# Expert weights in runs of 16384 bytes through 2 MB ring slots

## The chip, the cores and the metric

The kernel runs on one core of one Trainium2 chip. The metric is device time in microseconds, the median of three runs; lower is better. Times inside the program count from the start of the profiled span.

## The reference

One batch of 256 tokens of width 1024 goes through two blocks in float32. The first block is an RMS norm, a mixer (an mLSTM in chunks beside a pooled branch) and a mixture of experts; the second is attention and a gated delta rule side by side and a dense feed-forward. The change lies in the mixture of experts, which comes down to this:

```
logits = xt @ w_router + b_router                  # 256 tokens, 32 experts
top_vals, top_idx = top_k(logits, 4)               # each token goes to 4 experts
gate = min(xb @ w_gate[e] + b_gate[e], 7)          # w_gate[e], w_up[e], w_down[e]: 1024 x 1024 f32
up   = clip(xb @ w_up[e] + b_up[e], -7, 7)
y    = (gate * sigmoid(1.702 * gate) * (up + 1)) @ w_down[e] + b_down[e]
out  = sum over a token's experts of its gate weight * y
```

Three matrices of 4 MB for each of 32 experts make 384 MB of weights, and every byte is read once.

## The kernel before

All large weights come through a ring of slots in on-chip memory (class `Ring`, L25 to L89). A load is one entry of `jobs`, 1 MB for the expert weights. `order` (L39) gives a list of slot pools, and `add` (L42) hands each load the next pool of that list. `fill` (L47) issues loads strictly in the order of the list, all from SP's queue (L53): when the pool of the next load has no free slot, `fill` returns, and no later load is issued either, whatever is free elsewhere. `take` (L65) gives the oldest loaded piece to its user, and `refill` (L58), called in program order right behind the piece's last user, frees the slot and calls `fill` again. So the order of SP's loads is fixed when the program is built, and a load can wait on SP only for the last reader of the slot that it reuses.

Before the change there are nine pools: pool 0 with four slots of 2112 columns, pool 1 with eight of 2048, and seven pools of one slot of 2048, which are opened when the mixer's memory comes free (`open_late`, L859). Together that is 19 slots of 1 MB, and 156672 bytes of each partition. The pools are visited in a cycle of 19, so a load always takes the slot that the load 19 places before it had.

`plan_stream` (L482) lists the loads: ten of the mixer's input matrix and four of its output matrix, then the experts' in the order in which TensorE uses them: gate 0, up 0, gate 1, up 1, down 0, gate 2, up 2, down 1, and so on, four loads for each matrix. I number the experts' loads from load 0 (the first quarter of gate 0) to load 384 (the last quarter of down 31 comes as two halves). Expert 6's gate is loads 68 to 71, its up loads 72 to 75.

A load (`add_rows`, L78) takes 256 rows of a matrix, two neighbouring rows to a partition: a run of 8192 bytes in memory for each of 128 partitions. So the rows that one matmul contracts are every second row of 256, and the activations are arranged to match: `xn` is written with a stride at L829, `n2p` holds the norm's weights in that order (L226, L258), and `swiglu` writes with the same stride (L1262, L1268).

`experts` (L985) runs over the 32 experts. For each pair it gathers the tokens by one-hot matmuls (`group`, L1010; ps_x in the profile); for each expert it multiplies by gate and up (`up`, L1047; ps_g and ps_u), passes the result through `swiglu` on VectorE and ScalarE, transposes it (ps_t), multiplies by down one expert later (`down`, L1074; ps_y) and scatters the sums back. One load feeds four fp32 matmuls of 128x512, which the profile counts as eight.

Of the kernel before, what the change touches and what calls it, by code (L numbers as in the profile page):

```python
# [26 lines left out]
class Ring:  # L27

    def __init__(self, nc, sizes):
        self.nc, self.sizes, self.pools = nc, sizes, {}
        self.cols = (SLOT,) + (2048,) * (1 + LATE)
        self.jobs, self.tiles, self.sent, self.taken, self.freed = [], {}, 0, 0, 0
        self.where, self.held = [], [0] * len(sizes)
        self.limit = 1 << 30

    def order(self, cycle):
        self.cycle, self.at = cycle, 0  # L39

    def add(self, *pieces):
        self.where.append(self.cycle[self.at % len(self.cycle)])  # L42
        self.at += 1
        self.jobs.append(pieces)

    def fill(self, most=1 << 30):
        while self.sent < min(len(self.jobs), most, self.limit):  # L47
            i = self.where[self.sent]
            if i not in self.pools or self.held[i] == self.sizes[i]:
                return  # L50
            t = self.pools[i].tile([128, self.cols[i]], F32, tag="w", name="w")
            for view, src in self.jobs[self.sent]:
                self.nc.sync.dma_start(out=view(t), in_=src)  # L53
            self.held[i] += 1
            self.tiles[self.sent] = t
            self.sent += 1

    def refill(self):  # L58

        self.held[self.where[self.freed]] -= 1  # L60
        self.freed += 1
        self.fill()

    def take(self):
        t = self.tiles.pop(self.taken)  # L65
        self.taken += 1
        return t

    def add_cols(self, w, c0, n, kpt, k_total, cut=1):

# [6 lines left out]

    def add_rows(self, w):  # L78

        self.add((lambda t: t[:, :w.shape[0] // 128 * w.shape[1]], w.rearrange("(p i) c -> p (i c)", p=128)))  # L80

    def add_two_cols(self, w, c0, c1, n, kpt, k_total):
        for k0 in range(0, k_total, kpt):
# [9 lines left out]
class Kernel:  # L93
# [122 lines left out]
    def load_late(self):  # L216
        a, c = self.a, self.c
        self.param_rows("pe", ("norm2", a["norm2_g"].rearrange("o (k p) -> (o k) p", p=128), 8),
                        ("normmix", a["norm_mix_2"].rearrange("o (k p) -> (o k) p", p=128), 8),
                        ("normffn", a["norm_ffn_2"].rearrange("o (k p) -> (o k) p", p=128), 8),  # L220
                        ("normf", a["normf_g"].rearrange("(k p) -> k p", p=128), 8),
                        ("gdnn", a["gdn_norm_2"].rearrange("o (k p) -> (o k) p", p=128), 1))

        self.n2rows = self.rows.tile([4, 256], F32, name="n2rows")
        self.nc.sync.dma_start(out=self.n2rows, in_=a["norm2_g"].rearrange("o (j c) -> (o j) c", j=4))
        self.n2p = c.tile([128, 4, 2], F32, name="n2p")  # L226
# [23 lines left out]
    def param_cols(self, name, psp, tag):  # L250
# [3 lines left out]
        self.nc.vector.tensor_copy(self.pt[name], ps[:, :n])  # L254
        if name == "pb":
            ps = psp.tile([128, 512], F32, tag=tag, name="ps_p")
            for i in range(2):
                self.nc.tensor.transpose(ps[:, 4 * i:4 * i + 4], self.n2rows.rearrange("j (p i) -> j i p", i=2)[:, i, :],  # L258
                                         self.ident[:4, :4])
            self.nc.vector.tensor_copy(self.n2p, ps[:, 0:8].rearrange("p (i j) -> p j i", i=2))  # L260
# [221 lines left out]
    def plan_stream(self):  # L482
        a, r = self.a, self.ring
        if self.stop == "b2":
            return self.plan_stream2()
        r.order([0] * RING[0] + [1] * RING[1])
        w_in = a["w_in"][0]
        for c0, n in ((2048, 520), (0, 512), (512, 512), (1024, 512), (1536, 512)):
            r.add_cols(w_in, c0, n, 4, KD, 2 if c0 == 2048 else 1)
# [3 lines left out]
        if self.stop == "p1":  # L493
            return

        n = RING[0] + RING[1]
        first = [r.cycle[(r.at + i) % n] for i in range(n)]
        r.order(first[:n - 4] + list(range(2, 2 + MID)) + first[n - 4:] + list(range(2 + MID, 2 + LATE)))
# [9 lines left out]
        for e in range(E):  # L508
            if e + 1 < E:
                gu("w_gate", e + 1)  # L510
                gu("w_up", e + 1)
            if e + 1 < E:
                gu("w_down", e)
            else:
                w = a["w_down"][0, e]
                for k0 in range(0, D - 256, 256):
                    r.add_rows(w[k0:k0 + 256])
                for i in range(2):
                    r.add((lambda t: t[:, :D], w[D - 256:].rearrange("(p i) c -> i p c", i=2)[i]))
        if self.stop == "moe":  # L520
            return

# [23 lines left out]
    def mixer(self, block1):  # L546
        nc, tc, a = self.nc, self.tc, self.a
        v, g_ = nc.vector, nc.gpsimd
        with ExitStack() as ctx:
# [428 lines left out]
    def experts(self):  # L978
        nc, tc, a, x = self.nc, self.tc, self.a, self.x
        v = nc.vector  # L980
        with ExitStack() as ctx:
# [28 lines left out]
            def group(g):  # L1010
# [11 lines left out]
                for k in range(KD):  # L1022
                    ps = psx.tile([128, 512], F32, tag="x", name="ps_x")
                    for tb in range(2):
                        self.mm(ps[:, 0:GR * CAP], xn[:, tb, k * 128:(k + 1) * 128],
                                oh[:, tb].rearrange("p e s -> p (e s)"), start=tb == 0, stop=tb == 1)
                    self.act(xt[:, k, :], ps[:, 0:GR * CAP], scale=self.n2p[:, k // 2, k % 2:k % 2 + 1])
# [145 lines left out]
    def overflow_block(self, xn, e, psx, psg, psy, pst):  # L1173
# [16 lines left out]
        for k in range(KD):  # L1190
            for tb in range(2):
                self.mm(ps[:, k, :], xn[:, tb, k * 128:(k + 1) * 128], oh[:, tb, :], start=tb == 0, stop=tb == 1)
            self.act(xt[:, k, :], ps[:, k, :], scale=self.n2p[:, k // 2, k % 2:k % 2 + 1])
# [5 lines left out]

        def load(name, k):  # L1200
            w = q.tile([128, D], F32, tag="xg", name="ow")
            k0 = k // 2 * 256
            nc.sync.dma_start(out=w, in_=a[name][0][ds(e, 1), k0:k0 + 256, :].rearrange(
                "o (p i) c -> i p (o c)", i=2)[k % 2])
            return w

        gu = []
        for name, bn, tag, place in (("w_gate", "b_gate", "g", "gg"), ("w_up", "b_up", "u", "sc")):
# [11 lines left out]
            v.tensor_tensor(out=self.pairs(t), in0=self.plain(ps), in1=self.plain(b), op=OP.add)  # L1220
            gu.append(t)
        gg = gu[0]
        self.swiglu(gg, *gu, paired=True)
# [22 lines left out]
    def pairs(self, x):  # L1246

        return x.rearrange("p (a i q) -> p a q i", a=2, i=2)

    def plain(self, x):  # L1250
        return x.rearrange("p (a q i) -> p a q i", a=2, i=2)

    def swiglu(self, gg, pg, pu, paired=False):


        v = self.nc.vector
        t = self.mow.tile([128, 512], F32, tag="sg", name="sg", bufs=1)

        if paired:
# [5 lines left out]
        if paired:  # L1265
            v.tensor_scalar(out=t, in0=pu, scalar1=7.0, scalar2=-7.0, op0=OP.min, op1=OP.max)
        else:
            v.tensor_scalar(out=self.pairs(t), in0=self.plain(pu), scalar1=7.0, scalar2=-7.0, op0=OP.min, op1=OP.max)  # L1268
        v.scalar_tensor_tensor(out=gg, in0=t, scalar=1.0, in1=gg, op0=OP.add, op1=OP.mult)


# [834 lines left out]
```

## Time and profile before

| | |
|---|---|
| median of three runs | 1653.11 us (1653.06 to 1653.57) |
| the profiled execution's own time | 1652.3 us |
| its span | 1650.6 us |
| TensorE busy | 1567.6 us, 95% of the span |
| loads on SP's DMA queue | 506.01 MB, mean 308 GB/s over the span |
| mixer | 0 to about 125 us |
| experts | about 125 to 1054 us |
| second block | 1054 us to the end |

The span is cut into 40 slices of 41.3 us on the page. A digit is the busy share of an engine in tenths, and the GB/s line tells what the 16 DMA engines moved. Waits are put down to what came last; a wait of TensorE's weight load (PEld) for "DMA w" is one for a weight that has not landed.

### The profile page before, as it was taken

To read this page: it belongs to the slowest core of one execution; us is meant where nothing else is said; L and a number is where in the kernel's file an instruction comes from. 1 tells how busy PE (TensorE), PEld (TensorE's weight loads), DVE (VectorE), ACT (ScalarE), POOL (GpSimd) and SP (SyncE) were. 2 spreads that over 40 slices of the span, in tenths; PEclk is the share of its full clock that TensorE was granted. 3 is DMA by queue.
4 is the path that set the end of the run, shared out by engine and by line. 5 is a ranking of instruction groups with operands and counts; after the bars stand their busy time and mean duration, and the time that the engine had idled before them with its cause. 6 is when DMAs were issued, how large, how long until landed. Compare 5 with 4: busy or idle time off the path is not lost. (4 is left out here: it accounts for less than half of the span.)

```text
span 1650.6 us, 22396 instructions
## 1 busy us (share of the span) xinstructions
PE 1567.6 (95%) x8810; PEld 950.9 (58%) x8811; DVE 695.4 (42%) x1437; ACT 524.9 (32%) x1151; POOL 54.8 (3%) x124
## 2 busy tenths in 40 slices
PE   8999999999999999999999998799999999999997
PEld 8783333333333333333323322489888999989996
DVE  6862212212121212122121121388875376777775
ACT  4562111111111111111111110256663356565554
POOL 0100000000000000000000010000111010000000
PEclk9999999999999999999999999999999999999999
DMA  8878999999999999999999999644343333556551
GB/s 285 305 307 310 408 418 421 421 422 421 420 422 420 421 421 422 421 420 421 421 421 421 421 421 421 271 131 155 124 153 103 103 120 137 179 166 202 182 187 69
DMA packets 119235, 508.31 MB, mean 308 GB/s; under 512 B 10364, under 2 KB 33717, under 8 KB 70101
## 3 DMA queue, kind: packets, MB, share of 16 engines
q1 hardware_dynamic: 117284, 506.01, 77.8%
q8 instruction: 71, 1.16, 0.3%
q10 hardware_dynamic: 1840, 0.82, 0.2%
q14 instruction: 40, 0.32, 0.1%
HBM read 505.74 MB, written 1.05 MB: 307 GB/s over the span
## 5 line engine op out<-in xcount | busy, mean ns | idle before, releaser
L349 DVE TENSOR_TENSOR lo<-w,hi 128x512 fp32r<-128x512 f32 (+2 forms) x380 | 257.3, 691 | 56.9 <-PE ps_d L109 30.6
L1081 DVE COPY ht<-ps_t 128x512 f32<-128x512 f32 x32 | 22.1, 692 | 596.5 <-PE ps_t L1079 596.5
L109 PE MATMUL ps_y<-w,ht 128*64 128x512 f32 x1024 | 230.1, 597 | 29.8 <-DVE ht L1081 25.1
L106 ACT ACTIVATE hi<-w 128x512 fp32r<-128x512 f32 (+2 forms) x380 | 232.1, 628 | 74.8 <-PE ps_d L109 67.2
L109 PE MATMUL ps_g<-w,xg 128*64 128x512 f32 x1024 | 238.3, 600 | 6.1 <-DMA w<-in_w_gate_dram 4.9
L109 PE MATMUL ps_u<-w,xg 128*64 128x512 f32 x1024 | 238.0, 600 | 2.9 <-DMA w<-in_w_up_dram 2.8
L109 PEld LDWEIGHTS ps_y<-w,ht 128*64 128x64 f32 x1024 | 69.2, 136 | 170.0 <-issue 113.6
L106 ACT ACTIVATE xg<-ps_x,n2p 128x128 f32<-128x128 f32 x128 | 47.0, 368 | 334.3 <-PE ps_x L109 334.0
L109 PEld LDWEIGHTS ps_g<-w,xg 128*64 128x64 f32 x1024 | 67.1, 136 | 135.2 <-issue 101.0
L109 PEld LDWEIGHTS ps_u<-w,xg 128*64 128x64 f32 x1024 | 66.1, 136 | 116.6 <-issue 96.3
L109 PEld LDWEIGHTS ps_x<-oh,xn 128*128 128x128 f32 x512 | 68.7, 190 | 78.2 <-issue 64.7
L106 ACT ACTIVATE y<-ps_y 64x512 f32<-64x512 f32 x64 | 37.9, 592 | 186.7 <-PE ps_y L109 186.1
L109 PE MATMUL ps_x<-oh,xn 128*128 128x128 f32 x512 | 86.9, 294 | 0.8 <-DVE oh L1016 0.8
L106 ACT ACTIVATE sg<-gg 128x512 f32<-128x512 f32 x32 | 20.1, 629 | 200.4 <-DVE gg L1262 200.3
L1110 DVE TENSOR_TENSOR x<-x,ps_x 128x512 f32<-128x512 f32 x64 | 43.9, 686 | 91.9 <-PE ps_x L109 91.9
L109 PE MATMUL ps_d<-hnh,hi 128*128 128x256 f32 x448 | 77.7, 295 | 0.8 <-ACT hi L106 0.5
L109 PE MATMUL ps_d<-hnh,lo 128*128 128x256 f32 x448 | 71.5, 281 | 3.2 <-DVE lo L349 3.1
L109 PE MATMUL ps_d<-hnl,hi 128*128 128x256 f32 x448 | 71.1, 281 | 0.0
L109 PE MATMUL ps_x<-y,sc 128*128 128x512 f32 x128 | 59.2, 605 | 11.1 <-ACT y L106 11.1
L109 PEld LDWEIGHTS ps_d<-hnh,hi 128*128 128x128 f32 x448 | 61.5, 189 | 3.5 <-ACT hi L106 0.6
L109 PEld LDWEIGHTS ps_d<-hnh,lo 128*128 128x128 f32 x448 | 60.7, 188 | 4.0 <-DVE lo L349 3.8
L109 PEld LDWEIGHTS ps_d<-hnl,hi 128*128 128x128 f32 x448 | 60.8, 188 | 0.2
(435 smaller groups left out, 2079.3 us busy)
## 6 DMA issues: line engine op xcount, KB each, us to landing
w<-in_w_down_dram SPq DMA_DIRECT2D x137, 1024.0 KB
w<-in_w_gate_dram SPq DMA_DIRECT2D x128, 1024.0 KB
w<-in_w_up_dram SPq DMA_DIRECT2D x128, 1024.0 KB
w<-in_w_in_dram SPq DMA_DIRECT2D x40, 1024.0 KB
w<-in_w_up_dram SPq DMA_DIRECT2D x44, 512.0 KB
w<-in_w_out_dram SPq DMA_DIRECT2D x8, 1024.0 KB
w<-in_w_branch_gdn_dram SPq DMA_DIRECT2D x4, 1024.0 KB
w<-in_w_branch_fox_dram SPq DMA_DIRECT2D x4, 1024.0 KB
```

The source lines that it names most:

```text
L106: self.nc.scalar.activation(out=out, in_=in_, func=func, **kw)
L109: self.nc.tensor.matmul(out, lhsT=lhsT, rhs=rhs, start=start, stop=stop, **kw)
L349: nc.vector.tensor_tensor(out=lo[:, :n], in0=src, in1=hi[:, :n].bitcast(F32), op=OP.subtract)
L1081: v.tensor_copy(ht, ps)
L1110: v.tensor_tensor(out=o, in0=o, in1=ps, op=OP.add)
```

## The change

The 384 MB now go through slots of two sizes. Pool 1 has four slots of 4096 columns (2 MB) instead of eight of 2048, pools 2, 3 and 4 one slot of 4096 each, pool 5 one of 2048, and pool 0 stays with four of 2112. That is the same 156672 bytes: seven wide slots and five narrow ones. A wide load brings 512 rows, four neighbouring rows to a partition, as runs of 16384 bytes; its two halves are handed out one after the other, and the slot is free when both have been used. Where the next slot is a narrow one, the same 512 rows come as two loads of 8192-byte runs. All activations follow the new order of rows (stride four instead of two).

The visiting order is now a list written out, `MOE_RING`: its second list is gone through once, then its first list again and again. Each list has 24 entries: 14 wide and 10 narrow, 38 MB. Numbering by megabytes as before, a wide load has two numbers.

```diff
-    def order(self, cycle):
-        self.cycle, self.at = cycle, 0
+    def order(self, cycle, first=()):
+        self.cycle, self.first, self.at, self.part = cycle, first, 0, 0
+    def at_pool(self):
+        n = len(self.first)
+        return self.first[self.at] if self.at < n else self.cycle[(self.at - n) % len(self.cycle)]
+    def wide(self, i):
+        return self.cols[i] > SLOT
     def add(self, *pieces):
-        self.where.append(self.cycle[self.at % len(self.cycle)])
+        i = self.at_pool()
+        self.jobs.append((i, self.part, 1, pieces))
+        self.part = 1 - self.part if self.wide(i) else 0
+        self.at += not self.part
+    def add_both(self, piece):
+        i = self.at_pool()
+        assert self.wide(i) and not self.part
+        self.jobs.append((i, 0, 2, (piece,)))
         self.at += 1
-        self.jobs.append(pieces)
     def fill(self, most=1 << 30):
         while self.sent < min(len(self.jobs), most, self.limit):
-            i = self.where[self.sent]
-            if i not in self.pools or self.held[i] == self.sizes[i]:
-                return
...
+            i, part, n, pieces = self.jobs[self.sent]
+            if not part:
+                if i not in self.pools or self.held[i] == self.sizes[i]:
+                    return
+                self.tile = self.pools[i].tile([128, self.cols[i]], F32, tag="w", name="w")
+                self.held[i] += 1
...
     def refill(self):
-        self.held[self.where[self.freed]] -= 1
-        self.freed += 1
+        i, last = self.where.pop(0)
+        self.held[i] -= last
         self.fill()
...
     def add_rows(self, w):
-        self.add((lambda t: t[:, :w.shape[0] // 128 * w.shape[1]], w.rearrange("(p i) c -> p (i c)", p=128)))
+        n = w.shape[1]
+        rows = w.rearrange("(p i) c -> p (i c)", p=128)
+        if self.wide(self.at_pool()):
+            self.add_both((lambda t: t[:, :4 * n], rows))
+        else:
+            for i in (0, 2):
+                self.add((lambda t: t[:, :2 * n], rows[:, i * n:(i + 2) * n]))
...
-            for i in range(2):
-                self.nc.tensor.transpose(ps[:, 4 * i:4 * i + 4], self.n2rows.rearrange("j (p i) -> j i p", i=2)[:, i, :],
-                                         self.ident[:4, :4])
+            for i in range(4):
+                self.nc.tensor.transpose(ps[:, 2 * i:2 * i + 2], self.n2rows.rearrange("j (p i) -> j i p", i=4)[:, i, :],
+                                         self.ident[:2, :2])
...
-        r.order([0] * RING[0] + [1] * RING[1])
+        r.order([0] * 4 + [1] * 4)
...
+        r.order(*MOE_RING)
         def gu(name, e):
-            for k0 in range(0, D, 256):
-                r.add_rows(a[name][0, e, k0:k0 + 256])
+            for k0 in range(0, D, 512):
+                r.add_rows(a[name][0, e, k0:k0 + 512])
...
-                        self.act(self.xn[:, tb, c].rearrange("p (j i q) -> p j q i", j=2, i=2),
-                                 x[:, tb, c].rearrange("p (j q i) -> p j q i", j=2, i=2), scale=self.rs2[:, tb:tb + 1])
+                        self.act(self.xn[:, tb, c].rearrange("p (i q) -> p q i", i=4),
+                                 x[:, tb, c].rearrange("p (q i) -> p q i", i=4), scale=self.rs2[:, tb:tb + 1])
...
-            v.tensor_scalar(out=self.pairs(gg), in0=self.plain(pg), scalar1=7.0, scalar2=None, op0=OP.min)
+            v.tensor_scalar(out=self.fours(gg), in0=self.plain(pg), scalar1=7.0, scalar2=None, op0=OP.min)
...
-LATE, MID = 7, 4
-RING = (4, 8) + (1,) * LATE
+LATE, MID = 4, 2
+RING = (4, 4, 1, 1, 1, 1)
+COLS = (SLOT, 4096, 4096, 4096, 4096, 2048)
+MOE_RING = ([1, 1, 1, 2, 3, 1, 0, 0, 0, 0, 4, 1, 1, 1, 2, 3, 1, 5, 0, 0, 0, 4, 0, 5],
+            [0, 0, 1, 1, 1, 2, 3, 1, 0, 0, 4, 5, 0, 1, 1, 1, 2, 3, 1, 0, 0, 4, 0, 5])
```

On TensorE, ScalarE, VectorE and GpSimd the order of instructions stays as it is; only shapes change (two transposes of `n2rows` more, and the stride of `xn` and `swiglu`). What moves is SP's queue.

The first place is where the expert loads begin on SP, behind the mixer's output matrix: w is a slot, in_w_gate_dram and so on are the weights, and a row of 128x4096 is a wide load of 2 MB. Before:

```order
L53 DMA w<-in_w_out_dram 128x4x512 x4
L53 DMA w<-in_w_gate_dram 128x2048 x4
L53 DMA w<-in_w_up_dram 128x2048 x4
L53 DMA w<-in_w_gate_dram 128x2048 x4
L53 DMA w<-in_w_up_dram 128x2048 x4
L53 DMA w<-in_w_down_dram 128x2048 x4
```

And after:

```order
L72 DMA w<-in_w_out_dram 128x4x512 x4
L72 DMA w<-in_w_gate_dram 128x2048 x2
L72 DMA w<-in_w_gate_dram 128x4096
L72 DMA w<-in_w_up_dram 128x4096 x2
L72 DMA w<-in_w_gate_dram 128x4096 x2
L72 DMA w<-in_w_up_dram 128x4096
L72 DMA w<-in_w_up_dram 128x2048 x2
L72 DMA w<-in_w_down_dram 128x4096
L72 DMA w<-in_w_down_dram 128x2048 x2
```

The matrices come in the same order, in fewer and larger loads; the first two stay narrow.

The second place is the loads of expert 6's gate and up (loads 68 to 75) and the first of what follows, with what each waits for on SP. DMAHW0 to DMAHW7 are the eight semaphores that the loads take in turn, so that each load waits for the one eight before it; a PE wait is for the last reader of the slot. Before, one row is one number, 68 to 76:

```order
L53 DMA w<-in_w_gate_dram 128x2048 [waits DMAHW4_49,PE_49]
L53 DMA w<-in_w_gate_dram 128x2048 [waits DMAHW5_49,PE_49]
L53 DMA w<-in_w_gate_dram 128x2048 [waits DMAHW6_49,PE_49]
L53 DMA w<-in_w_gate_dram 128x2048 [waits DMAHW7_49,PE_49]
L53 DMA w<-in_w_up_dram 128x2048 [waits DMAHW0_49,PE_49]
L53 DMA w<-in_w_up_dram 128x2048 [waits DMAHW1_49,PE_49]
L53 DMA w<-in_w_up_dram 128x2048 [waits DMAHW2_49,PE_49]
L53 DMA w<-in_w_up_dram 128x2048 [waits DMAHW3_49,PE_49]
L53 DMA w<-in_w_down_dram 128x2048 [waits DMAHW4_49,PE_49]
```

After, the rows are 68, 69, 70, 71, 72 with 73, 74, 75, and 76 with 77. They are entries 18 to 24 of the repeated list (pools 5, 0, 0, 0, 4, 0, 5) and entry 1 of its next round:

```order
L72 DMA w<-in_w_gate_dram 128x2048 [waits DMAHW1_49]
L72 DMA w<-in_w_gate_dram 128x2048 [waits DMAHW2_49,PE_49]
L72 DMA w<-in_w_gate_dram 128x2048 [waits DMAHW3_49,PE_49]
L72 DMA w<-in_w_gate_dram 128x2048 [waits DMAHW4_49,PE_49]
L72 DMA w<-in_w_up_dram 128x4096 [waits DMAHW5_49,PE_49]
L72 DMA w<-in_w_up_dram 128x2048 [waits DMAHW6_49]
L72 DMA w<-in_w_up_dram 128x2048 [waits DMAHW7_49,DMAHW1_49,PE_49]
L72 DMA w<-in_w_down_dram 128x4096 [waits DMAHW0_49]
```

Load 75 now waits for a second load's semaphore, DMAHW1, which is that of the first row here, load 68: both go into the one slot of pool 5.

## Rows read from the trace of the kernel before

**Rows 1.** The page: TensorE busy in tenths and GB/s, 40 slices of 41.3 us.

```profile
PE   8999999999999999999999998799999999999997
...
GB/s 285 305 307 310 408 418 421 421 422 421 420 422 420 421 421 422 421 420 421 421 421 421 421 421 421 271 131 155 124 153 103 103 120 137 179 166 202 182 187 69
```

**Rows 2.** Stretches: busy us (instructions) of five engines, granted clock, DMA share, GB/s.

```profile
125.00:213.00 88.00, 84.62 (x391) 33.31 (x391) 19.71 (x41) 16.51 (x39) 0.82 (x4) 1.00 0.93 365
213.00:780.00 567.00, 544.41 (x2480) 204.18 (x2480) 117.80 (x180) 76.70 (x170) 4.09 (x20) 1.00 1.01 421
780.00:1054.00 274.00, 250.17 (x1104) 86.29 (x1103) 52.32 (x78) 30.58 (x66) 6.32 (x10) 1.00 1.00 416
```

**Rows 3.** Waits of the weight load, 213 to 780 us: total us, times, longest.

```profile
PEld ps_y L109 <- DMA w<-in_w_up_dram: 1.7, 6, 0.3
```

**Rows 4.** The same waits, 780 to 1054 us.

```profile
PEld ps_y L109 <- DMA w<-in_w_down_dram: 21.2, 25, 1.7
PEld ps_u L109 <- DMA w<-in_w_up_dram: 8.9, 10, 1.4
PEld ps_g L109 <- DMA w<-in_w_gate_dram: 8.4, 7, 1.4
```

**Rows 5.** Timeline of TensorE, expert 6 and 8: start, length, line, instruction, count.

```profile
293.95 3.60 PE L109 MATMUL ps_g<-w,xg 128*64 128x512 f32 x16
...
350.67 2.74 PE L109 MATMUL ps_g<-w,xg 128*64 128x512 f32 x12
```

**Rows 6.** DMA, 300 to 400 us: packets and GB/s, and share of 16 engines.

```profile
DMA packets 5779, 42.13 MB, mean 421 GB/s; under 512 B 639, under 2 KB 639, under 8 KB 639
...
q1 hardware_dynamic: 5776, 42.08, 101.2%
```

**Rows 7.** DMA, 27 to 52 us, the mixer's loads (runs of 2048 bytes).

```profile
DMA packets 4845, 9.73 MB, mean 389 GB/s; under 512 B 156, under 2 KB 156, under 8 KB 4842
...
q1 hardware_dynamic: 4842, 9.70, 104.3%
```

**Rows 8.** Timeline of SP's loads, 268 to 300 us.

```profile
271.59 0.33 SPq L53 DMA_DIRECT2D w<-in_w_up_dram  x1
274.10 6.50 SPq L53 DMA_DIRECT2D w<-in_w_down_dram  x4
297.59 0.33 SPq L53 DMA_DIRECT2D w<-in_w_down_dram  x1
```

**Rows 9.** DMA, 0 to 277 us: bytes, and loads issued by then.

```profile
q1 hardware_dynamic: 20064, 95.27, 87.7%
...
w<-in_w_gate_dram SPq DMA_DIRECT2D x28, 1024.0 KB
w<-in_w_up_dram SPq DMA_DIRECT2D x28, 1024.0 KB
w<-in_w_down_dram SPq DMA_DIRECT2D x22, 1024.0 KB
```

**Rows 10.** Timeline of SP, 69 to 72 us, DMA engines idle before.

```profile
70.03 0.33 SPq L53 DMA_DIRECT2D w<-in_w_up_dram  x1
```

**Rows 11.** DMA, 70 to 72 us: GB/s in 40 slices of 0.05 us.

```profile
GB/s 0 0 0 0 0 0 0 0 0 0 0 0 0 0 0 0 0 0 0 0 1147 164 0 164 492 164 0 164 492 0 0 0 0 0 0 164 0 0 0 0
```

**Rows 12.** ScalarE, 119 to 125 us: count, busy us, mean ns, idle before.

```profile
L106 ACT ACTIVATE xn<-x,nr 128x512 f32<-128x512 f32 x4 | 4.1, 1172 | 0.0
L106 ACT ACTIVATE ht<-ps_b 128x512 f32<-128x512 f32 x2 | 1.1, 594 | 0.7 <-PE ps_b L879 0.7
```

**Rows 13.** Timeline, expert 31: swiglu on VectorE, transposes, last load's matmuls.

```profile
1035.45 1.05 DVE L1262 TENSOR_SCALAR gg<-ps_g 128x512 f32<-128x512 f32 x1
...
1039.09 0.69 DVE L1269 SCALAR_TENSOR_TENSOR gg<-sg,gg 128x512 f32<-128x512 f32 x1
...
1043.81 0.42 PEld L1079 LDWEIGHTS ps_t<-ident,gg 128*128 128x128 f32 x4 [0.81 <-issue]
...
1049.62 3.65 PE L109 MATMUL ps_y<-w,ht 128*64 128x512 f32 x16 [0.41 <-DMA w<-in_w_down_dram]
```

More of the change, by code (lines that the diff above doesn't have):

```diff
@@ L32, in __init__ @@
         self.nc, self.sizes, self.pools = nc, sizes, {}
-        self.cols = (SLOT,) + (2048,) * (1 + LATE)
-        self.jobs, self.tiles, self.sent, self.taken, self.freed = [], {}, 0, 0, 0
+        self.cols = COLS
+        self.jobs, self.tiles, self.sent = [], [], 0
         self.where, self.held = [], [0] * len(sizes)
         self.limit = 1 << 30
-    def order(self, cycle):
-        self.cycle, self.at = cycle, 0
-    def add(self, *pieces):
-        self.where.append(self.cycle[self.at % len(self.cycle)])
+    def order(self, cycle, first=()):
+        self.cycle, self.first, self.at, self.part = cycle, first, 0, 0
@@ L43, in add @@
         self.at += 1
-        self.jobs.append(pieces)
     def fill(self, most=1 << 30):
         while self.sent < min(len(self.jobs), most, self.limit):
-            i = self.where[self.sent]
-            if i not in self.pools or self.held[i] == self.sizes[i]:
-                return
[L51 to L55, printed above, removed]
+            i, part, n, pieces = self.jobs[self.sent]
@@ new lines, in fill @@
+            if not part:
[3 more added lines that the diff above has]
+                self.held[i] += 1
+            t = self.tile
+            for view, src in pieces:
+                self.nc.sync.dma_start(out=view(t[:, part * 2048:] if n == 1 else t), in_=src)
+            for j in range(part, part + n):
+                self.tiles.append(t[:, j * 2048:] if self.wide(i) else t)
+                self.where.append((i, j == 1 or not self.wide(i)))
@@ L56, in fill @@
             self.sent += 1
     def refill(self):
-        self.held[self.where[self.freed]] -= 1
-        self.freed += 1
+        i, last = self.where.pop(0)
+        self.held[i] -= last
         self.fill()
     def take(self):
-        t = self.tiles.pop(self.taken)
-        self.taken += 1
-        return t
+        return self.tiles.pop(0)
     def add_cols(self, w, c0, n, kpt, k_total, cut=1):
@@ L222, in load_late @@
                         ("gdnn", a["gdn_norm_2"].rearrange("o (k p) -> (o k) p", p=128), 1))
-        self.n2rows = self.rows.tile([4, 256], F32, name="n2rows")
-        self.nc.sync.dma_start(out=self.n2rows, in_=a["norm2_g"].rearrange("o (j c) -> (o j) c", j=4))
-        self.n2p = c.tile([128, 4, 2], F32, name="n2p")
+        self.n2rows = self.rows.tile([2, 512], F32, name="n2rows")
+        self.nc.sync.dma_start(out=self.n2rows, in_=a["norm2_g"].rearrange("o (j c) -> (o j) c", j=2))
+        self.n2p = c.tile([128, 2, 4], F32, name="n2p")
         self.param_rows("pb", ("gconv", a["gdn_conv_w_2"].rearrange("o i (k p) -> (o i k) p", p=128), 96))
@@ L256, in param_cols @@
             ps = psp.tile([128, 512], F32, tag=tag, name="ps_p")
-            for i in range(2):
-                self.nc.tensor.transpose(ps[:, 4 * i:4 * i + 4], self.n2rows.rearrange("j (p i) -> j i p", i=2)[:, i, :],
-                                         self.ident[:4, :4])
-            self.nc.vector.tensor_copy(self.n2p, ps[:, 0:8].rearrange("p (i j) -> p j i", i=2))
+            for i in range(4):
+                self.nc.tensor.transpose(ps[:, 2 * i:2 * i + 2], self.n2rows.rearrange("j (p i) -> j i p", i=4)[:, i, :],
+                                         self.ident[:2, :2])
+            self.nc.vector.tensor_copy(self.n2p, ps[:, 0:8].rearrange("p (i j) -> p j i", i=4))
         if name == "pe":
@@ L494, in plan_stream @@
             return
-        n = RING[0] + RING[1]
-        first = [r.cycle[(r.at + i) % n] for i in range(n)]
-        r.order(first[:n - 4] + list(range(2, 2 + MID)) + first[n - 4:] + list(range(2 + MID, 2 + LATE)))
+        r.order(*MOE_RING)
         def gu(name, e):
-            for k0 in range(0, D, 256):
-                r.add_rows(a[name][0, e, k0:k0 + 256])
+            for k0 in range(0, D, 512):
+                r.add_rows(a[name][0, e, k0:k0 + 512])
         gu("w_gate", 0)
@@ L515, in plan_stream @@
                 w = a["w_down"][0, e]
[L516 to L519, printed above, removed]
+                r.add_rows(w[0:512])
+                w = w[512:].rearrange("(p i) c -> p (i c)", p=128)
+                for i, m in ((0, 2), (2, 1), (3, 1)):
+                    r.add((lambda t, m=m: t[:, :m * D], w[:, i * D:(i + m) * D]))
         if self.stop == "moe":
@@ L1026, in group @@
                                 oh[:, tb].rearrange("p e s -> p (e s)"), start=tb == 0, stop=tb == 1)
-                    self.act(xt[:, k, :], ps[:, 0:GR * CAP], scale=self.n2p[:, k // 2, k % 2:k % 2 + 1])
+                    self.act(xt[:, k, :], ps[:, 0:GR * CAP], scale=self.n2p[:, k // 4, k % 4:k % 4 + 1])
                     yield
@@ L1192, in overflow_block @@
                 self.mm(ps[:, k, :], xn[:, tb, k * 128:(k + 1) * 128], oh[:, tb, :], start=tb == 0, stop=tb == 1)
-            self.act(xt[:, k, :], ps[:, k, :], scale=self.n2p[:, k // 2, k % 2:k % 2 + 1])
+            self.act(xt[:, k, :], ps[:, k, :], scale=self.n2p[:, k // 4, k % 4:k % 4 + 1])
         s = q.tile([128, T], F32, tag="oh", name="osc", bufs=1)
@@ L1201, in load @@
             w = q.tile([128, D], F32, tag="xg", name="ow")
-            k0 = k // 2 * 256
-            nc.sync.dma_start(out=w, in_=a[name][0][ds(e, 1), k0:k0 + 256, :].rearrange(
-                "o (p i) c -> i p (o c)", i=2)[k % 2])
+            k0 = k // 4 * 512
+            nc.sync.dma_start(out=w, in_=a[name][0][ds(e, 1), k0:k0 + 512, :].rearrange(
+                "o (p i) c -> i p (o c)", i=4)[k % 4])
             return w
@@ L1219, in overflow_block @@
             t = q.tile([128, 512], F32, tag=place, name="og_u", bufs=1 if place == "gg" else None)
-            v.tensor_tensor(out=self.pairs(t), in0=self.plain(ps), in1=self.plain(b), op=OP.add)
+            v.tensor_tensor(out=self.fours(t), in0=self.plain(ps), in1=self.plain(b), op=OP.add)
             gu.append(t)
         gg = gu[0]
-        self.swiglu(gg, *gu, paired=True)
+        self.swiglu(gg, *gu, done=True)
         ps = pst.tile([128, 512], F32, tag="t", name="ps_t")
@@ L1244, in overflow_block, with fours, swiglu @@
                 v.tensor_tensor(out=o, in0=o, in1=ps, op=OP.add)
-    def pairs(self, x):
-        return x.rearrange("p (a i q) -> p a q i", a=2, i=2)
+    def fours(self, x):
+        return x.rearrange("p (i q) -> p q i", i=4)
     def plain(self, x):
-        return x.rearrange("p (a q i) -> p a q i", a=2, i=2)
-    def swiglu(self, gg, pg, pu, paired=False):
+        return x.rearrange("p (q i) -> p q i", i=4)
+    def swiglu(self, gg, pg, pu, done=False):
         v = self.nc.vector
         t = self.mow.tile([128, 512], F32, tag="sg", name="sg", bufs=1)
-        if paired:
+        if done:
             v.tensor_scalar(out=gg, in0=pg, scalar1=7.0, scalar2=None, op0=OP.min)
         else:
-            v.tensor_scalar(out=self.pairs(gg), in0=self.plain(pg), scalar1=7.0, scalar2=None, op0=OP.min)
+            v.tensor_scalar(out=self.fours(gg), in0=self.plain(pg), scalar1=7.0, scalar2=None, op0=OP.min)
         self.act(t, gg, AF.Sigmoid, scale=1.702)
         v.tensor_tensor(out=gg, in0=gg, in1=t, op=OP.mult)
-        if paired:
+        if done:
             v.tensor_scalar(out=t, in0=pu, scalar1=7.0, scalar2=-7.0, op0=OP.min, op1=OP.max)
         else:
-            v.tensor_scalar(out=self.pairs(t), in0=self.plain(pu), scalar1=7.0, scalar2=-7.0, op0=OP.min, op1=OP.max)
+            v.tensor_scalar(out=self.fours(t), in0=self.plain(pu), scalar1=7.0, scalar2=-7.0, op0=OP.min, op1=OP.max)
         v.scalar_tensor_tensor(out=gg, in0=t, scalar=1.0, in1=gg, op0=OP.add, op1=OP.mult)
```

## The prediction

> **What bounds the kernel now.** The page's two long lines come first [rows 1]: TensorE is busy nearly everywhere, so it looks like the bound, but from slice 5 to slice 25 the DMA engines stand at 420 to 422 GB/s without a dent. The stretches tell which of the two ends last [rows 2]: TensorE's busy share in the experts is 96% from 213 to 780 us and 91% from 780 to 1054 us, while DMA stays full (share 1.01 and 1.00). The weight load's waits for weights say why [rows 3, 4]: 1.7 us in the first of these stretches, 38.5 us (21.2 + 8.9 + 8.4) in the second. So TensorE first lives on the 19 MB in the ring and uses it up, since it is a little quicker than the DMA engines. Expert 6's gate starts at 293.95 us and expert 8's at 350.67 [rows 5], 56.7 us for 24 loads, 2.363 us a load. The DMA engines need 1.0486 MB / 421 GB/s = 2.491 us [rows 6]. From about 800 us the ring is empty, and TensorE waits for each load. The experts' end is therefore the DMA engines' end: the time at which they began to run without a pause, plus the bytes left at their pace. A pause of theirs in the middle is paid in full at the end, unless TensorE still had to spare, and it has nothing to spare at 800 us.
>
> **What the longer runs bring.** A run of 16384 bytes isn't in the trace; runs of 2048 and 8192 are, both with the engines full (shares over 100%): 389 GB/s [rows 7] and 421 GB/s [rows 6], that is 2.696 and 2.491 us for 1.0486 MB. Each of 16 engines moves that as 32 packets or as 8. So 24 packets cost 0.205 us, 8.5 ns each, and what is left without packets is 2.422 us. With 4 packets it would be 2.456: 34 ns less for a MB in a wide load, my value, since it continues the two rows. The lower end is no gain at all, 0 (the long run is cut up, or the rate has another limit); the upper one is all eight packets' cost gone, 68 ns. Below zero I keep 34 ns of loss with little weight: from 2 to 8 KB the rate only rises. In the list of 24 entries 28 of 38 MB are wide, 74%.
>
> In these rows a packet costs 8.5 ns. The Trainium skill ("DMA: Bandwidth & Descriptors", section "Why small descriptors are slow (HBM only)") tells of a fixed overhead of about 3 cycles for a packet beside 32-byte beats. An estimate from it: 515 cycles for 512 beats in place of 518, 14 ns a MB, and by it the sum would be 1670.3 us, which lies in the first rival's bounds below and has a part of its chance. From 2 to 8 KB the rule gives 3.5%, where the rows have 8%, so the rows decide. The same page (section "Where 436 GB/s comes from") has 435 GB/s as the ports' ceiling, by which a MB can't gain over 81 ns.
>
> **What the order of the slots costs.** SP issues loads strictly in the list's order, so a load whose slot is still in use holds back all behind it. Before, every load takes the slot of the load 19 places ahead, and can be issued when that has been used. I went through the new lists with that rule. Wide loads may start when the user is 16 MB behind, narrow ones mostly at 18, a small loss while the ring is full. One place stands out: the repeated list has six narrow entries among its last seven (5, 0, 0, 0, 4, 0, 5), and there are five narrow slots. The second 5 falls on load 75, the last quarter of expert 6's up; the first was load 68, the first quarter of expert 6's own gate. SP's rows show that tie: load 75 waits for the semaphore of load 68's DMA and for TensorE. So load 75 can only be issued when TensorE has used load 68, when it is 6 loads ahead instead of 18, and loads 76 and on wait behind it on SP, where nothing else stands until the experts end.
>
> When is that? Load 68 is the first half of expert 6's first gate row: 293.95 plus half of 3.60 = 295.8 us [rows 5]. TensorE gets there at the same time as before, since it waited for no weights until then [rows 3]. From the issue to the first bytes it takes 1.0 us (issued at 70.03, bytes from slice 21 of 40, 71.0 us) [rows 10, 11]. So load 75's bytes start at 296.8 us. Before, it was issued at 271.59, as the last row ahead of the down loads [rows 8]. Its bytes started when all ahead of it had passed: 75 loads (78.64 MB), the mixer's matrices (10.52 + 4.19), x, the pool weights and the rest (2.03), 95.38 MB. By 277 us 95.27 MB had passed [rows 9], so 277.3 us. The DMA engines are 296.8 - 277.3 = 19.5 us late. What happens to the loads ahead of 75 is hidden in this pause: the coarser slots at the start may put load 74 off by some us, but they have 19 to spend.
>
> TensorE doesn't feel it at once: at 296 us loads 69 to 74 are in the ring, and load 75 is needed only some 15 us later (7 loads at 2.363 less what it has begun). But the reserve that lasted to 800 us is smaller by 12 loads, so it lasts to some time between 400 and 500 us, and from there TensorE goes at the DMA's pace.
>
> Does the tie bite again 38 MB later, load 113 on load 106? TensorE, still at its own pace, has used 106 at 295.8 + 38 x 2.363 = 385.6, and the load could start at 386.6. The DMA engines come to it at 296.8 + 38 x (2.491 - 0.74 x 0.034) = 390.5. They are 4 us late already, so there is no second pause; with 68 ns saved it would be 389.5, still none.
>
> **The rest.** From load 75 on 309 MB are left, 228 of them wide: 228 x 0.034 = 7.8 us back. For the restart of an idle DMA queue and because a wide load can be used only when all its 2 MB have landed I add 1.0 us; the bounds are 0 and one load of 1 MB, 2.5 us (the last MB still comes in halves). ScalarE's four writes of xn take 1172 ns with stride two where a write of the same size without a stride takes 594 [rows 12]; they stand ahead of the first gather and shift load 68's use with them. With stride four they can come down to 594 (2.3 us less) or double again (4.7 us more); I take no change, as the nearest row is a strided one. In swiglu the two strided steps are hidden: expert 31's chain takes from 1035.45 to 1039.8 and its transposes start at 1043.81 [rows 13], so if both doubled (2.1 us) they still would be. Two transposes more for n2p lie in the mixer, under 0.2 us. Fewer loads on SP save nothing, as no one waits for SP's issue.
>
> **Sum.** 19.5 - 7.8 + 1.0 = 12.7 us on the profiled execution's own 1652.3 us, 1665.0. The median of the runs shown is 0.8 above that execution, so 1665.8 us.
>
> **The rivals.**
> - *The long runs bring nothing* (under 17 ns a MB): 19.5 + 1.0, 1673.6 us. For it: 421 GB/s is already flat within 2 GB/s over 20 slices, as a hard limit would be. Against it: the rise from 389 to 421.
> - *They bring far more* (over 51 ns): 19.5 - 15.5 + 1.0 = 5.0, 1658.1 us. For it: in the stream the engines are over 100% busy, so packets queue on each other, and fewer may queue less. Against it: nothing in the rows shows such a step.
> - *The tie doesn't bite* (faster, not slower): load 75 is issued before load 68 is used, or DMA has such a backlog at 277 us that the pause is covered. Then the pace decides from about 190 us on [rows 1]: some 344 MB, 254 wide, 8.6 us back. Against that the full ring's start: wide loads issued 16 instead of 18 ahead, up to two loads of 2.49 us late. 1653.1 - 8.6 + 5.0 = 1649.5 us; it turns faster when the late start costs less than 8.6. For it: the rows of SP are an order and not a time. Against it: loads 76 and on stand behind load 75 on the same queue, so the engines have nothing else to move.
>
> **How the numbers follow.** Forecast, pause and 17 to 51 ns: 0.60. No gain: 0.17. Far more gain: 0.15. No pause: 0.08. The first runs from +8.9 to +16.6, 1662 to 1670. The range takes in the second and third and a part of the stride's bounds: 1656 to 1676; outside are the case without a pause and single extremes, under 2 in 10. A measurement of this kernel tells 0.2%, 3.3 us, from no change. Faster by more: most of the case without a pause, 0.06. Within: the rest of it and the upper end of far more gain, 0.05. Slower: 0.89.
>
> **What would show it.** In the new profile the GB/s line falls to some 330 to 350 in slices 7 and 8 of 40 (248 to 330 us), with an empty stretch from about 280 to 297 us, and SP's load of the last up quarter of expert 6 stands at about 296 us instead of 272. Expert 6's gate still starts at 293.95. Later slices stand near 425 GB/s. Waits of the weight load for DMA begin between 400 and 500 us instead of 800, and the experts end near 1066 instead of 1053 us. Large packets take about twice those of before. The second block is as long as before. I am wrong if no DMA pause is seen near 290 us, if slices behind it stand at 421 or above 430, or if expert 0 starts more than 2 us off its time.

## The result, and the profile after

The changed kernel takes 1666.01 us in the median of four runs (1664.98 to 1667.53); the kernel before took 1653.09 us beside it (1652.65 to 1653.57). The ratio is 1.0079, with a 95% interval of 1.0061 to 1.0096: 12.9 us slower. The profiled executions differ by nearly as much, 12.7 us, with spans of 1663.3 and 1650.6 us.

The page of the kernel after, in 40 slices of 41.6 us, answers to [rows 1].

```profile
PE   8999999999999999999999998799999999999997
...
GB/s 284 284 299 282 410 426 334 348 428 424 426 426 425 425 428 425 426 427 426 426 423 427 424 426 426 323 127 153 127 128 126 92 113 152 174 169 190 191 182 72
```

TensorE's line is the same to the digit. The other line has a dent in slices 7 and 8 (334 and 348), and behind it it stands some 5 GB/s higher than before, for 17 slices. Both parts of the change can be read here, the loss in two slices and the gain in the rest.

The stretches (length, then busy us of PE, PEld, DVE, ACT and POOL, granted clock, DMA share, GB/s) put a size on it; the third runs to the new end of the experts [rows 2].

```profile
125.00:213.00 88.00, 83.83 (x391) 33.44 (x392) 19.50 (x44) 16.95 (x40) 0.82 (x4) 1.00 0.88 351
213.00:780.00 567.00, 534.87 (x2419) 199.42 (x2419) 112.51 (x174) 73.90 (x164) 4.07 (x20) 0.99 0.98 413
780.00:1067.00 287.00, 261.36 (x1171) 95.39 (x1167) 58.27 (x85) 33.38 (x72) 6.30 (x10) 1.00 1.00 420
1067.00:1663.00 596.00, 573.35 (x4128) 527.32 (x4128) 418.02 (x904) 331.45 (x733) 32.21 (x43) 0.99 0.44 145
```

The second stretch lost 8 GB/s and TensorE did 61 matmuls fewer in it. The last row is the second block, 596 us long as before (1054 to 1650 us).

Where the dent comes from is seen on SP's queue from 262 to 302 us [rows 8], and on the DMA engines from 280 to 297 us (40 slices of 0.43 us).

```profile
266.75 30.87 SPq L72 DMA_DIRECT2D w<-in_w_up_dram  x3
297.67 0.90 SPq L72 DMA_DIRECT2D w<-in_w_down_dram  x2
298.61 1.40 SPq L72 DMA_DIRECT2D w<-in_w_gate_dram  x2
```

```profile
GB/s 405 405 328 270 289 193 135 77 77 19 0 0 0 0 0 0 0 0 0 0 0 0 0 0 0 0 0 0 0 0 0 0 0 0 0 39 0 0 0 0
DMA packets 130, 0.95 MB, mean 56 GB/s; under 512 B 23, under 2 KB 23, under 8 KB 23
```

The first row holds the last three loads of expert 6's up, the last of them load 75. The group ends at 297.62, so load 75 was issued at about 297.3. The engines run dry from 281 us and are empty from 284.

TensorE gives the time of that issue: expert 6's gate, before at 293.95 [rows 5].

```profile
295.36 3.60 PE L133 MATMUL ps_g<-w,xg 128*64 128x512 f32 x16
```

Half of it, the part that uses load 68, ends at 297.16, a tenth of a microsecond ahead of load 75's issue. With the 1.0 us to the first bytes [rows 10, 11] they come at 298.3, 21.0 us later than the 277.3 worked out for before.

The DMA engines from 300 to 400 us [rows 6]: 42.59 MB in place of 42.13, in 3680 packets in place of 5779.

```profile
DMA packets 3680, 42.59 MB, mean 426 GB/s; under 512 B 405, under 2 KB 405, under 8 KB 405
...
q1 hardware_dynamic: 3677, 42.54, 100.8%
```

Over 300 to 900 us the kernel after moves 255.11 MB on that queue, and the kernel before 252.32. That is 2.466 against 2.493 us for a MB of 1.0486, 27 ns less on average, 37 ns for a MB in a wide load at 74% wide.

```profile
q1 hardware_dynamic: 22072, 255.11, 100.6%
```

The waits of the weight load for weights (us in total, times, longest) from 500 to 600 us, and from 780 to 1067 us [rows 4]. Before, all of 213 to 780 had 3.4 us of them, none longer than 0.3: the 1.7 us of [rows 3] and two smaller groups of 1.1 and 0.6 us, which [rows 3] doesn't show.

```profile
PEld ps_g L133 <- DMA w<-in_w_gate_dram: 2.9, 3, 2.1
PEld ps_y L133 <- DMA w<-in_w_down_dram: 1.2, 2, 0.8
...
PEld ps_g L133 <- DMA w<-in_w_gate_dram: 6.2, 4, 3.8
PEld ps_y L133 <- DMA w<-in_w_down_dram: 5.1, 7, 1.7
PEld ps_u L133 <- DMA w<-in_w_up_dram: 2.6, 3, 2.0
```

The last down product ends the experts: at 1059.00 + 7.19 = 1066.19 us, before at 1049.62 + 3.65 = 1053.27 [rows 13]. The difference is 12.9 us, all of the result.

```profile
1059.00 7.19 PE L133 MATMUL ps_y<-w,ht 128*64 128x512 f32 x32 [2.20 <-SPq L1181]
```

### The profile page after: what moved, and what is told of

The parts are those of the page before. It is cut to its first block, busy times and chain, and to the rows that moved or that the text cites. A ratio compares the mean times of both kernels' runs of the same rounds, so it can differ in the third digit from the quotient of the medians.

```text
span 1663.3 us, 22039 instructions
## 1 busy us (share of the span) xinstructions
PE 1569.7 (94%) x8812; PEld 956.2 (57%) x8813; DVE 695.0 (42%) x1437; ACT 524.6 (32%) x1151; POOL 54.1 (3%) x124
## 5 line engine op out<-in xcount | busy, mean ns | idle before, releaser
L133 PE MATMUL ps_g<-w,xg 128*64 128x512 f32 x1024 | 239.2, 603 | 17.8 <-DMA w<-in_w_gate_dram 16.6
```

Of the source, the lines that this page charges most:

```text
L133: self.nc.tensor.matmul(out, lhsT=lhsT, rhs=rhs, start=start, stop=stop, **kw)
```

## The experiments

The theory: load 75, tied to load 68's slot, stops the DMA engines for some 20 us; the end of the experts moves by all of it; and the length of the runs, nothing else, gives back 28 to 38 ns a MB. Against it stand the coarse slots (2 MB come free and land at once), the size of the loads, and the pause as something that TensorE's stock covers.

**The list without the tie.** The slots and runs stay, only the list changes.

```diff
-MOE_RING = ([1, 1, 1, 2, 3, 1, 0, 0, 0, 0, 4, 1, 1, 1, 2, 3, 1, 5, 0, 0, 0, 4, 0, 5],
-            [0, 0, 1, 1, 1, 2, 3, 1, 0, 0, 4, 5, 0, 1, 1, 1, 2, 3, 1, 0, 0, 4, 0, 5])
+NARROW, ROUND = [0, 0, 0, 0, 5], [1, 1, 1, 2, 3, 1, None, None, 4, None, None]
...
+def even_ring():
+    first, k, out = [0, 0], 2, []
+    for _ in range(5):
+        for p in ROUND:
+            if p is None:
+                p, k = NARROW[k % 5], k + 1
+            out.append(p)
+    return out, first
...
+MOE_RING = even_ring()
```

A round has seven wide and four narrow entries (the expectation below miscounts them as six and five), so 14 of 18 MB are wide, 78% in place of 74.

> The changed kernel with another list of ring entries: two narrow entries, then rounds of eleven entries (six wide slots, five narrow ones) in which the narrow slots stand in the order 0, 0, 0, 0, 5, so that each slot is named again only after at least 16 other loads, and load 75 no longer shares the slot of load 68. Runs of 16384 bytes in 14 of 18 MB of the ring, as before 75 to 78 of 100 MB of the stream. Theory (the pause is the tie of load 75 on load 68; long runs give back 28 to 38 ns per MB): the empty stretch from 284 to 298 us goes, the slices 7 and 8 stand at 420 GB/s and more, and the time falls by 18 to 22 us against the changed kernel, to 1645 to 1650 us, 3 to 8 us under the kernel before. Rival A (loads of 2 MB and their coarse slots cost the time whatever the order of the list): the dip stays, perhaps spread over 200 to 300 us, and the time stays at 1660 to 1668 us. Rival B (the gain came from the pause itself, not from the runs): the pause goes and the pace returns to 2.49 us per MB, time 1655 to 1660 us.

Measured: 1649.01 us, ratio to the kernel before 0.9978 (0.9969 to 0.9987). The page's GB/s line and the window from 276 to 300 us:

```profile
GB/s 287 286 304 273 409 426 426 426 425 425 425 428 425 426 426 428 427 426 425 425 427 426 425 426 426 241 153 155 118 139 103 103 125 132 179 166 203 181 189 67
...
DMA packets 805, 10.31 MB, mean 429 GB/s; under 512 B 92, under 2 KB 92, under 8 KB 92
```

No dent, the same pace as after the change, and no DMA wait of the weight load at all from 213 to 780 us. With that the sign turns: some 17 us against the changed kernel hang on the order of the list (17.0 between the medians; the two were not measured side by side, and by their distances from the kernel before, +12.9 and -3.7, it is 16.6). That is a little less than the 18 to 22 expected. Rivals A and B are out.

**The tie alone.** The kernel before, with one entry changed; 14 loads of the mixer come first in `jobs`.

```diff
-        self.where.append(self.cycle[self.at % len(self.cycle)])
+        n = len(self.jobs)
+        self.where.append(self.where[n - 7] if n == 14 + 75 else self.cycle[self.at % len(self.cycle)])
```

> The kernel before (1 MB loads in runs of 8192 bytes) with one entry of its list changed: load 75 takes the slot that load 68 holds, so that it can be issued only once load 68 has been used, and every load behind it on SP's queue waits with it. Theory (the tie alone makes the pause, and every microsecond of it reaches the end of the experts): first bytes of load 75 at 297 us in place of 277 us, no bytes from about 284 us until then, the pace afterwards 2.49 us per MB as before, the experts' end 19 to 21 us later, time 1672 to 1675 us. Rival A (the pause comes from the 2 MB slots and not from the tie): no pause or one of 1 to 3 us, time 1653 to 1656 us. Rival C (the pause is made up later, since the ring is full and TensorE waits): the pause is there and the time is 1653 to 1662 us.

Measured: 1671.87 us, ratio 1.0119 (1.0105 to 1.0134), 19.1 us over the kernel before (1652.75 on that chip). SP's queue, and the DMA engines from 276 to 300 us:

```profile
263.38 32.58 SPq L54 DMA_DIRECT2D w<-in_w_up_dram  x3
296.01 2.15 SPq L54 DMA_DIRECT2D w<-in_w_down_dram  x4
```

```profile
GB/s 369 287 164 96 41 0 0 0 0 0 0 0 0 0 0 0 0 0 0 0 0 0 0 0 0 0 0 0 0 0 27 0 0 0 109 164 382 423 423 410
```

The same hole, without a single wide slot or long run. In the second fence, slice 34 (from 296.4 us) has the first bytes behind load 75's issue; a finer view puts them at 296.5, 19.2 us behind the 277.3 of before. The experts end 19.4 us later than before:

```profile
1069.05 3.65 PE L110 MATMUL ps_y<-w,ht 128*64 128x512 f32 x16 [0.57 <-DMA w<-in_w_down_dram]
```

So the pause is paid whole, and it costs what was forecast for it, 19.5 us, to within 0.4. The time is a hair under the 1672 to 1675 expected. Rivals A and C are out.

**The tie with short runs.** The changed kernel, each wide load as two transfers of 8192-byte runs.

```diff
+                if n == 2:
+                    for h in (0, 1):
+                        c = slice(h * 2048, (h + 1) * 2048)
+                        self.nc.sync.dma_start(out=view(t)[:, c], in_=src[:, c])
+                    continue
```

> The changed kernel with each 2 MB load issued as two 1 MB loads of 8192-byte runs into the two halves of the same slot, in the same order and with the tie of load 75 on load 68 kept. Theory (the pace comes from the length of the runs): the pause at 284 to 298 us stays as it is, the pace goes back from 2.466 to 2.49 us per MB, the experts' end 8 to 9 us later than in the changed kernel, time 1673 to 1675 us. Rival (the pace comes from fewer, larger loads in one transfer order or from the ring's arrangement, not from the runs): as the changed kernel, 1665 to 1668 us.

Measured: 1672.81 us, ratio 1.0126 (1.0112 to 1.0141), 6.8 us over the changed kernel (7.1 by their distances from the kernel before), where 7 to 9 were expected. The dent stays and the pace is that of before:

```profile
GB/s 289 281 318 274 406 421 320 368 421 421 421 422 421 422 421 422 421 421 421 421 421 421 422 421 421 345 127 139 131 135 127 78 125 142 175 173 185 198 180 73
```

This is 0.9 us over the tie alone: beside the tie, coarse slots cost hardly anything more. That their lateness falls into the pause is the reading of it.

**Neither tie nor long runs.** The even list with the same edit as in the third experiment.

> The list without the tie (two narrow entries, then rounds of eleven) and each 2 MB load issued as two 1 MB loads of 8192-byte runs: the coarse slots alone, without the tie and without the long runs. Theory: no pause; what is left against the kernel before is that a slot is named again after 16 to 17 loads in place of 18 and comes free 2 MB at a time, which while the ring is full delays the issue by up to 5 us: time 1653 to 1659 us, 8 to 9 us above the same list with long runs. Rival A (coarse slots make the loss): 1665 to 1675 us. Rival B (the runs give nothing without the pause): the same time as the list without the tie and with long runs.

Measured: 1656.88 us, ratio 1.0034 (1.0010 to 1.0058). So without the tie the coarse slots, with whatever else the change does to the start, do cost something, 4.1 us over the kernel before, and the long runs are worth 7.9 (1656.9 to 1649.0). The stretch from 125 to 213 us, against 365 GB/s [rows 2]:

```profile
125.00:213.00 88.00, 84.26 (x389) 33.69 (x390) 19.52 (x43) 16.52 (x39) 0.82 (x4) 1.00 0.88 348
```

17 GB/s less over 88 us are 1.5 MB, 3.6 us at 421 GB/s. Another 0.7 MB was missing before that; what SP's queue moved from 0 to 213 us, first this kernel, then the kernel before, is 2.2 MB apart, 5.3 us:

```profile
q1 hardware_dynamic: 16079, 66.28, 80.5%
```

```profile
q1 hardware_dynamic: 16386, 68.50, 83.7%
```

From 213 us on the pace is 421 GB/s in both, so the loss lies at the start. It stands unchanged at the end of the experts, 1054.87 + 3.65 = 1058.52 us, 5.25 later than 1053.27; the time is only 4.1 us longer, since the rest of that execution is 1.1 us shorter.

```profile
1054.87 3.65 PE L138 MATMUL ps_y<-w,ht 128*64 128x512 f32 x16 [0.47 <-DMA w<-in_w_down_dram]
```

**The size of a load or the length of a run.** The even list with 2 MB loads, rows laid out as before, so that each load has two runs of 8192 bytes in a partition.

```diff
-            self.add_both((lambda t: t[:, :4 * n], rows))
+            self.add_both((lambda t: t[:, :4 * n].rearrange("p (b x) -> p b x", b=2),
+                           w.rearrange("(b p i) c -> p b (i c)", b=2, p=128)))
```

> The list without the tie, with 2 MB loads as one transfer each, but with the rows laid out as in the kernel before, so that a partition gets two separate runs of 8192 bytes where it got one of 16384. It parts the size of a load from the length of its runs. Theory (the gain comes from the length of the runs): pace 2.49 us per MB, packets of 8 KB at 309 to 314 ns, time 1655 to 1659 us, as with the 2 MB loads cut into two 1 MB loads (1656.9). Rival (the gain comes from half as many, twice as large loads): pace 2.466 us per MB and 1647 to 1651 us, as with the long runs (1649.0).

Measured: 1658.16 us, ratio 1.0034 (1.0021 to 1.0047). The DMA engines from 650 to 1000 us, first this kernel, then the kernel before:

```profile
q1 hardware_dynamic: 19351, 147.22, 101.1%
...
w<-in_w_down_dram SPq DMA_DIRECT2D x20, 2048.0 KB
```

```profile
q1 hardware_dynamic: 20213, 147.19, 101.1%
```

Loads of twice the size move the same bytes in the same time. What gains is the run, not the load.

**The tie where little lies in store.** As in the second experiment, with `n == 14 + 303`.

> The kernel before with the same tie, seven loads back, at load 303 (on load 296) in place of load 75 (on load 68): there TensorE has used up the ring and takes each load soon after it lands. Theory (a tie costs the time between the hand-over that the DMA engines need and the one that the list gives them, and only where landed loads lie unused in the ring): load 296 is used before the queue behind it has emptied, the DMA engines do not stop, time 1652 to 1655 us. Rival (a tie seven loads back costs some 15 to 20 us wherever it stands): 1668 to 1673 us.

Measured: 1652.93 us, ratio 1.0002 (0.9992 to 1.0012). From 830 to 880 us:

```profile
DMA packets 2893, 21.08 MB, mean 422 GB/s; under 512 B 322, under 2 KB 322, under 8 KB 322
```

No gap, though the tie holds load 303 back. It was the last row of its group on SP, first here, then in the kernel before; with 0.33 us for that row, it was issued at 839.8 us in place of 832.0:

```profile
824.14 16.02 SPq L54 DMA_DIRECT2D w<-in_w_up_dram  x4
```

```profile
824.52 7.79 SPq L53 DMA_DIRECT2D w<-in_w_up_dram  x4
```

By 840 us the queue had moved 332.05 MB, which with the prediction's 16.74 MB ahead of the experts is 300.7 loads (an estimate). So loads 301 and 302 still kept the engines busy when load 303 came. The same seven places cost 19 us at 297 us and nothing here. SP's waits in the kernel before tell the two places apart. From 255 to 300 us they are all for TensorE (35.9 us in total), so the slots set the time of an issue, 19 places back. From 820 to 850 us they are for DMA but for 0.3 us (25.2), that is for the load eight before, so the tie asks for a load only one place nearer, though for its use and not its landing. In that stretch it adds this one wait:

```profile
SPq L54 <- PE ps_g L110: 5.8, 1, 5.8
```

**Only wide slots, late.** The even list for ten rounds, then the seven wide slots in turn; the diff is against the list without the tie, which ran again beside it.

```diff
-    first, k, out = [0, 0], 2, []
-    for _ in range(5):
+    first, k = [0, 0], 2
+    for _ in range(10):
...
-            out.append(p)
-    return out, first
+            first.append(p)
+    return [1, 1, 1, 2, 3, 1, 4], first
```

> The list without the tie for its first ten rounds (180 MB), then only the seven wide slots in turn: 14 MB of ring, every load 2 MB in runs of 16384 bytes. Theory: by then fewer than 14 MB lie landed and unused, so the smaller ring costs nothing, and the last quarter of the loads, some 50 MB, gains 28 to 38 ns per MB too: 1.4 to 1.9 us below the list without the tie, 1646.5 to 1648 us. Rival (the ring is still needed whole after 180 MB): a stall after about 570 us, time 1650 to 1660 us.

> The list without the tie once more, on the chip of these three, so that they can be told from it by less than one per thousand: 1647.5 to 1650.5 us, 0.15 to 0.3 per cent under the kernel before.

Measured on one chip: 1647.41 us with only wide slots late (ratio 0.9982, 0.9963 to 1.0002, runs from 1643.2 to 1658.1), 1650.33 us for the list without the tie (0.9981, 0.9972 to 0.9990). The ring of 14 MB brings no stall, and the pace is higher; from 650 to 1000 us, first with only wide slots, then the first run of the list without the tie:

```profile
q1 hardware_dynamic: 10261, 149.46, 100.4%
```

```profile
q1 hardware_dynamic: 12532, 148.99, 100.6%
```

A MB takes 2.456 us where every load is wide, 2.493 before (147.19 MB), 38 ns less. That it is a faster kernel than the list without the tie isn't shown: the medians say 2.9 us, but four of its twelve runs took 1655.0 to 1658.1 us, and its interval against the kernel before takes in no change. What is shown twice is that the list without the tie is faster than the kernel before, by about 0.2%; it is faster than the changed kernel by some 1%.

## Why the prediction was right, and where it was off

The four kernels that differ only in list and runs stand in one table (medians in us). The changed kernel was measured apart from the other three; the kernel before took 1653.1 us beside it and 1652.8 beside them.

| | tie of load 75 | no tie |
|---|---|---|
| 16384-byte runs | 1666.0 (the change) | 1649.0 |
| 8192-byte runs | 1672.8 | 1656.9 |

- **The bound.** Right: the DMA engines' pause reached the experts' end whole (second experiment: 19.2 us there, 19.4 at the experts' end, 19.1 in the time). TensorE's stock postpones it and doesn't pay it.
- **The tie.** Right in place and cause, 1.5 us too small: 21.0 instead of 19.5. TensorE came to load 68 1.4 us later. I had expert 6's gate at 293.95, and it was at 295.36; expert 0 began 1.4 us late already. That comes from the mixer, and most of it from 61 to 70 us, where the granted clock differs (columns as above). First the kernel after, then the kernel before, then the kernel with only wide slots late, whose mixer is that of the kernel after:

```profile
61.00:64.00 3.00, 3.00 (x7) 1.84 (x7) 2.93 (x7) 1.44 (x5) 0.00 (x0) 0.50 1.03 440
64.00:67.00 3.00, 3.00 (x7) 1.83 (x7) 2.54 (x6) 1.77 (x6) 0.54 (x1) 0.50 0.16 66
```

```profile
61.00:64.00 3.00, 3.00 (x8) 1.89 (x8) 2.93 (x7) 1.91 (x6) 0.18 (x1) 0.56 1.03 429
64.00:67.00 3.00, 3.00 (x11) 1.74 (x10) 2.71 (x6) 2.13 (x6) 0.65 (x2) 0.87 0.92 380
```

```profile
61.00:64.00 3.00, 3.00 (x12) 2.06 (x12) 2.93 (x6) 2.49 (x7) 0.42 (x1) 1.00 0.99 421
64.00:67.00 3.00, 3.00 (x12) 1.81 (x11) 2.93 (x7) 2.94 (x9) 0.51 (x2) 1.00 0.27 115
```

   In each of the three TensorE was busy for only 0.9 to 1.2 of the 3 us before these rows (58 to 61 us). With the clock at half (1.2 GHz) for longer the same matmuls take longer; at full clock throughout (2.4 GHz), expert 0 began at 123.60 us, before the change at 125.69, after it at 127.12:

```profile
127.12 1.94 PE L133 MATMUL ps_g<-w,xg 128*64 128x512 f32 x8
```

   Not all of the 1.4 us is the clock's. Five other executions with the changed mixer and three with the mixer of before have the same mean clock from 61 to 67 us, 0.72 (after: 0.50); the five began expert 0 at 125.98 to 126.51, the three at 125.45 to 125.94. So some 0.6 us come with the changed kernel's own start, by a way that no run here settles, and some 0.8 with the clock. Why it falls for longer in one execution isn't settled either.
- **The runs.** Right in kind, a little small: 37 to 38 ns a wide MB where the two rows gave 34. Over the 309 MB that is 309 x 0.0273 = 8.4 us, forecast 7.8. The estimate from the Trainium skill ("DMA: Bandwidth & Descriptors", section "Why small descriptors are slow (HBM only)"), 14 ns a MB, is not borne out by these 37 to 38.
- **Restart and coarser landing.** Forecast 1.0 us. What is left over at the experts' end is 12.9 - 21.0 + 8.4 = 0.3, and tie with short runs against tie alone gives 0.9.
- **No second pause at load 113.** Right: the slices behind the dent have none. The start's lateness costs at most 0.9 us beside the pause, as supposed; without the pause it is 4.1 us in the time and 5.25 at the experts' end, near the 5.0 of the rival without a tie, whose 1649.5 us the list without the tie met with 1649.0.
- **The edits at nothing.** The writes of `xn` at stride four take 1170 ns, before 1172 [rows 12], so the bounds of -2.3 and +4.7 us fall away; the first strided step of `swiglu` (gg) takes 1049 ns in place of 1056 (medians).

```profile
L130 ACT ACTIVATE xn<-x,nr 128x512 f32<-128x512 f32 x4 | 4.0, 1170 | 0.0
```

- **Small miss of a sign.** DMA waits were to begin between 400 and 500 us; by 500 there are 1.3 us, with one wait of 0.7 as the longest, and the first real ones lie between 500 and 600. The forecast gave no sum for this; its 15 us in hand, used up at 2.491 - 2.363 = 0.13 us a load, would last some 115 loads or 270 us, to about 570 us (an estimate).

The total came within 0.2 us of the median by luck, as these misses nearly cancel: the pause cost 1.5 us more than forecast, the runs gave 0.6 more back and the restart cost 0.7 less. Each term by itself was right to 1.5 us.

## What to carry to other kernels

In a ring that one queue fills in order, count for each load how many loads ahead its slot was last used: one entry with a short distance stops all behind it. The cost is what of its later issue the engines' queue doesn't cover: here 25.7 us later (297.3 in place of 271.6) with 21.0 lost where the ring was full, and 7.8 us later with nothing lost where it was nearly used up. Where the transfer engines bound a long stretch, time lost early in it is paid at its end, even when the consumer shows no wait for 200 us. Check an order of slots apart from the length of the runs, since here a gain of some 8 us from the one lay under a loss of some 17 us from the other.

## What the runs showed of the hardware

- Run length and load size are separate. With 8192-byte runs 1 MB and 2 MB loads move 147.19 and 147.22 MB in 350 us; with 16384-byte runs it is 149.46. From 2048 to 8192 bytes a packet more had cost 8.5 ns; from 8192 to 16384 it is 38 ns for four, 9.5 each.
- ScalarE's write of 128x512 that deals its elements out in turn to four places 128 elements apart (the stride of four) takes as long as one between two such places, 1170 against 1172 ns. A write of that size in order takes 594 in another instruction, which reads ps_b [rows 12].
- The start of the experts moved by 3.5 us (123.60 to 127.12) between executions with the same mixer, the first at a mean granted clock of 1.00 from 61 to 67 us and the last at 0.50; five at 0.72 lie between (125.98 to 126.51). For a change of 0.2% such a shift has to be read off before the rest is compared.
